# A decoder layer's MLP: the second product as seven block products instead of eight

## The chip, the cores and the metric

The kernel runs on one core of a Trainium2 chip, in float32. The time is device microseconds of one execution. The profile is one execution recorded by the hardware, and its times are counted from the first instruction.

## The reference, cut to what matters

One decoder layer on 1024 tokens of width 1024; the token mixers ahead of the MLP (an RWKV-7 recurrence and a differential attention) are left out here.

```
x = x + merged @ w_out[i]                                       # out projection
h = rmsnorm(x, norm_mlp_g[i])
x = x + jnp.square(jax.nn.relu(h @ w_ff1[i])) @ w_ff2[i]        # MLP, hidden width 4096
gate = jax.nn.sigmoid(rmsnorm(x, norm_ple_g[i]) @ w_ple_gate[i])
x = x + (p[i] @ w_ple[i]) * gate                                # gate stage
return rmsnorm(x, final_norm_g)
```

## The kernel before, in words

**Split operands.** Every large product runs on TensorE in a float32 form that keeps few bits. So each operand is split in two: `hi`, a cast by ScalarE, and `lo`, the rest, a subtraction on VectorE or GpSimd (`split`). `mm3` then issues three matmuls per pair of tiles, hi by hi, hi by lo and lo by hi, each 128x128 by 128x512.

**Order.** The code is recorded once and a scheduler places the instructions on the queue of each engine: PE (TensorE), DVE (VectorE), ACT (ScalarE), POOL (GpSimd), and SP, which issues all the DMAs. Each queue runs in its order. A tile's space is taken again once its last reader is done.

**The stages that matter.**
- *Out projection* (`out_proj`): two halves of columns, eight tiles of 128 tokens (`j`) each. In the second half `norm(j)` norms a finished tile, transposes it on TensorE into `h2`, and makes from the even tiles the operands `hb[0]` and `hb[1]` of the first MLP product, and from each pair of tiles four differences.
- *First MLP product* (`phase_ff1`): 16 pairs `g` of 128 hidden rows. The product of 2x2 blocks is already done with seven block products (Strassen's way in Winograd's form), in the order 0, 5, 1, 6, 4, 3, 2, each 12 matmuls. The moving operands `hb[i]` for i above 1 are made during pair 0 (`moving`). To cover that, products 0 and 1 of the first `AHEAD` pairs run first. The block sums go through relu and square and are stored in `dr_hid` in memory.
- *Second MLP product* (`phase_ff2`): eight groups of four tiles of 128 hidden rows. A group loads four tiles of hidden (`h0r` to `h3r`) and four of weights (`w0r` to `w3r`), splits all, and for each of the eight token tiles issues 2 halves x 4 x 3 = 24 matmuls; VectorE adds the result to `x2` (L1120).
- *Gate stage* (`phase_ple`): the gate's weights are loaded and split during the second MLP product, then each token tile in turn is normed (`normed`), multiplied, gated and stored.

Of the kernel before, what the change touches and what calls it, by code (L numbers as in the profile page):

```python
# [79 lines left out]
class Kern:  # L80
    def __init__(self, tc, A, out):
        self.tc, self.nc, self.A, self.out = tc, tc.nc, A, out
        self.raws = {}
# [79 lines left out]
    def run(self):  # L163
        nc, tc, A = self.nc, self.tc, self.A
        with ExitStack() as es:
# [13 lines left out]
            self.dr_hid = dr.tile([DFF // P, P, T], F32, name="dr_hid")  # L179
# [10 lines left out]
            with ExitStack() as right:  # L190
# [3 lines left out]
                self.f1w = opener(mid)("f1w", 5)  # L194
# [527 lines left out]
    def project(self, gw, pd, mA):  # L722
# [159 lines left out]
    def out_proj(self, pool, mA):  # L882
# [9 lines left out]
        def norm(j, xj):  # L892

            xn = self.norm_scale(xj, (nw, nw))
            nc.sync.dma_start(self.dr_x2[j, :, H:D], xj[:, H:D])
            col = lambda c: slice(c * H + j // 2 * P, c * H + (j // 2 + 1) * P)
            blk = lambda kk, c: self.h2[:, 4 * kk:4 * kk + 4, col(c)]
            for q in range(2):
# [4 lines left out]
                if j % 2 == 0:  # L903
                    self.split([t[:, :, col(0)] for t in self.hb[q]], blk(q, 0), q)
            if j % 2:
# [3 lines left out]
                sub(blk(0, 0), blk(0, 1), blk(0, 0))  # L909
                sub(t1, blk(1, 1), blk(0, 0))  # L910
                sub(blk(1, 0), blk(1, 0), t1)
                sub(blk(0, 1), blk(1, 1), blk(0, 1))

        for c in range(2):
            cols = slice(c * H, c * H + H)
            ws = [self.weights(wp, A["w_out"][k][:, cols], [P, H], "wo", lo="gv"[k % 2], raw_bufs=2) for k in range(KD)]
            for j in range(NT):
# [22 lines left out]
                if j:  # L940
# [4 lines left out]
        self.first = [self.ff1_split(self.raws[0, 0][:, 4 * i:4 * i + 4, :], i) for i in range(2)]  # L945
# [18 lines left out]

    def phase_ff1(self, pool):
# [8 lines left out]

        nc, A = self.nc, self.A
        hp, w1, wk = pool("f1h", 1), pool("f1s", 4), pool("f1k", 6)
# [7 lines left out]
        sums = lambda name, **k: wk.tile([P, H], F32, tag="o", name=name, **k)  # L984
        n = DFF // P // 2
# [12 lines left out]
        def stationary(g, order):  # L998
# [9 lines left out]
            for i in order:  # L1008
# [14 lines left out]
                yield i, self.ff1_split(src, g < 2 or i in (0, 1))  # L1023

        def store(g, m, c, src, on_scalar=False):

            o = sums("o")
            if on_scalar:
                nc.scalar.activation(o, src, AF.Relu)
                src = o  # L1030
            nc.vector.scalar_tensor_tensor(o, src, 0.0, src, op0=ALU.max, op1=ALU.mult)  # L1031
            nc.sync.dma_start(self.dr_hid[2 * g + m, :, c * H:c * H + H], o)

        def product(b, i, w, first):
            for k in range(4):
                self.mm3(b, w[0][:, k, :], w[1][:, k, :], hb[i][0][:, k, :], hb[i][1][:, k, :], first and k == 0, k == 3, not first)

        p0 = {}
        for g in range(AHEAD):
            ws = self.first if g == 0 else [self.ff1_split(raws[g, 0][:, 4 * i:4 * i + 4, :], True) for i in range(2)]  # L1040
# [5 lines left out]
            bs = [PT(), PT()]  # L1046
            for i in range(2):
                product(bs[i], i, ws[i], True)
                if i == 0:
                    p0[g] = wk.tile([P, H], F32, tag=f"p0{g}", name="p0", bufs=1)  # L1050
                    nc.scalar.copy(p0[g], bs[0])
            x = sums("x00")
            nc.vector.tensor_tensor(x, p0[g], bs[1], op=ALU.add)
            store(g, 0, 0, x)
        for g in range(n):
# [12 lines left out]
            for i, w in stationary(g, [i for i in ORDER if g >= AHEAD or i > 1]):  # L1068
# [4 lines left out]
                product(b, i, w, first)  # L1073
# [5 lines left out]
                elif i == 1:  # L1079
                    store(g, 0, 0, b, True)  # L1080
                elif i == 6:
                    plus("v", sb["u"], b)
                elif i == 4:
                    store(g, 1, 1, plus("x11", sb["v"], b))
                elif i == 3:
                    store(g, 1, 0, plus("x10", sb["u"], b))
                else:
                    store(g, 0, 1, plus("x01", sb["u"], b))

    def phase_ff2(self, pool):  # L1090

        nc, A = self.nc, self.A
        G = 4

        raw, ops = pool("f2r", 3), [pool(f"f2g{g}", 1) for g in range(2)]
        p2 = pool("f2p", 4, space=PSUM)

        def part(p, src, tag, v):
            r = raw.tile([P, D], F32, tag=tag[0] + "r", name=tag + "r")
            nc.sync.dma_start(r, src)  # L1100
            parts = [p.tile([P, D], F32R, tag=f"{tag}{n}", name=f"{tag}{n}") for n in ("hi", "lo")]
            self.split(parts, r, v)
            return parts

        n = DFF // P // G
        load = lambda g: [(part(ops[g % 2], self.dr_hid[G * g + i], f"h{i}", False), part(ops[g % 2], A["w_ff2"][G * g + i], f"w{i}", i % 2))
                          for i in range(G)]
        nxt = load(0)
        for j in range(NT):
            nc.sync.dma_start(self.x2[:, j, :], self.dr_x2[j])  # L1110
        for g in range(n):
            ws, nxt = nxt, load(g + 1) if g + 1 < n else None
            for j in range(NT):
                tok = slice(j % 2 * H + j // 2 * P, j % 2 * H + (j // 2 + 1) * P)
                pt = p2.tile([P, D], F32, tag="p2", name="p2")
                for c in range(2):
                    cols = slice(c * H, c * H + H)
                    for i, (hh, w) in enumerate(ws):
                        self.mm3(pt[:, cols], hh[0][:, tok], hh[1][:, tok], w[0][:, cols], w[1][:, cols], i == 0, i == G - 1)
                nc.vector.tensor_tensor(self.x2[:, j, :], self.x2[:, j, :], pt, op=ALU.add)  # L1120


    def phase_ple(self, pool, rpool):
        nc, A = self.nc, self.A

        wgs = [pool("plg", 1), rpool("plgr", 1)]
        left = 6
        nk, hp = pool("pln", 2), pool("plh", 2)
        wk, one = pool("plw", 2), pool("plo", 1)
# [3 lines left out]
        raw = lambda name, *shape: nk.tile([P, *shape], F32, tag="raw", name=name, bufs=3)  # L1133

        def normed(j):
            h = [hp.tile([P, KD, P], F32R, tag=f"h{i}", name=f"h{i}") for i in range(2)]
            self.norm_turn(self.norm_scale(self.x2[:, j, :], (nk, nk), raw("xn", D)), "norm_ple_g", h, (nk, nk, ps))
            return h

# [119 lines left out]
```

## Time and profile before

| | |
|---|---|
| time, median of 3 runs (lowest to highest) | 1786.38 us (1785.12 to 1790.37) |
| the profiled execution: its own time, its span | 1785.24 us, 1783.5 us |
| TensorE busy (matmuls) | 1735.6 us, 97% of the span |
| VectorE, ScalarE, GpSimd busy | 1031.8, 631.0, 388.9 us |
| mean granted TensorE clock | 0.997 of full speed |

The own time is 1.7 us above the span: what lies around the first and last instruction. An engine's busy time counts what it executes; the rest of its span it waits for another engine or a DMA.

### The profile page before, as it was taken

To read this page: it belongs to the slowest core of one execution; us is meant where nothing else is said; L and a number is where in the kernel's file an instruction comes from. 1 tells how busy PE (TensorE), PEld (TensorE's weight loads), DVE (VectorE), ACT (ScalarE), POOL (GpSimd) and SP (SyncE) were. 2 spreads that over 40 slices of the span, in tenths; PEclk is the share of its full clock that TensorE was granted. 3 is DMA by queue.
4 is the path that set the end of the run, shared out by engine and by line. 5 is a ranking of instruction groups with operands and counts; after the bars stand their busy time and mean duration, and the time that the engine had idled before them with its cause. 6 is when DMAs were issued, how large, how long until landed. Compare 5 with 4: busy or idle time off the path is not lost. (4 is left out here: it accounts for less than half of the span.)

```text
span 1783.5 us, 24054 instructions
## 1 busy us (share of the span) xinstructions
PE 1735.6 (97%) x9002; PEld 1424.3 (80%) x9002; DVE 1031.8 (58%) x2051; ACT 631.0 (35%) x1196; POOL 388.9 (22%) x321
## 2 busy tenths in 40 slices
PE   7999999999999999999999999999999999999998
PEld 7778877878877887788777778888878888888787
DVE  6357576676576564867547986566543333332653
ACT  5231452352353254766223422222231111112432
POOL 4000011010010010111502033333373333334000
PEclk9999999999999999999999999999999999999999
DMA  4323222221322318642543233333293222203101
GB/s 160 96 71 117 74 77 83 66 77 54 95 78 67 112 72 241 221 130 84 189 159 107 95 124 119 113 101 119 89 337 123 95 95 95 95 24 118 48 36 47
DMA packets 98276, 191.66 MB, mean 107 GB/s; under 512 B 34032, under 2 KB 35056, under 8 KB 98160
## 3 DMA queue, kind: packets, MB, share of 16 engines
q1 hardware_dynamic: 98160, 190.13, 32.4%
q8 instruction: 71, 1.16, 0.3%
q14 instruction: 45, 0.37, 0.1%
HBM read 138.19 MB, written 51.90 MB: 107 GB/s over the span
## 5 line engine op out<-in xcount | busy, mean ns | idle before, releaser
L158 PE MATMUL pd<-hT,w_hi 128*128 128x512 f32 (+1 forms) x688 | 274.4, 399 | 1.8 <-DVE stlo L333 1.6
L160 PE MATMUL pd<-hT,w_lo 128*128 128x512 f32 (+1 forms) x688 | 269.0, 391 | 0.0
L159 PE MATMUL pd<-hT,w_hi 128*128 128x512 f32 (+1 forms) x688 | 268.8, 391 | 0.0
L1120 DVE TENSOR_TENSOR x<-x,p 128x1024 f32<-128x1024 f32 x64 | 78.1, 1221 | 206.6 <-PE p L160 206.5
L158 PEld LDWEIGHTS pd<-hT,w_hi 128*128 128x128 f32 x688 | 129.9, 189 | 26.2 <-DVE stlo L333 2.0
L160 PEld LDWEIGHTS pd<-hT,w_lo 128*128 128x128 f32 x688 | 129.7, 188 | 24.2 <-issue 0.2
L159 PEld LDWEIGHTS pd<-hT,w_hi 128*128 128x128 f32 x688 | 129.9, 189 | 22.8 <-issue 1.0
L628 POOL COPY XV<-vt 64x128 f32<-64x128 f32 x64 | 21.0, 328 | 461.9 <-PE ps L642 365.5
L953 POOL TENSOR_TENSOR wlo<-s,whi 128x512 fp32r<-128x512 f32 x56 | 75.8, 1356 | 185.6 <-ACT whi L952 185.6
L152 DVE TENSOR_TENSOR w_lo<-w_raw,w_hi 128x1024 fp32r<-128x1024 f32 x42 | 51.3, 1221 | 72.3 <-ACT w_hi L151 71.9
L952 ACT CAST whi<-s 128x512 fp32r<-128x512 f32 x64 | 39.5, 622 | 120.6 <-PE p L159 97.6
L952 ACT CAST h0hi<-h0r 128x1024 fp32r<-128x1024 f32 x8 | 8.4, 1052 | 191.0 <-PE p L159 148.3
L151 ACT CAST w_hi<-w_raw 128x1024 fp32r<-128x1024 f32 x42 | 44.1, 1050 | 88.2 <-PE pd L159 81.8
L839 DVE CUSTOM_DVE_ANT_0 sc<-ps,tab 128x512 f32<-128x512 f32 (+3 forms) x96 | 50.7, 552 | 23.6 <-PE ps L837 23.0
L1031 DVE SCALAR_TENSOR_TENSOR o<-x 128x512 f32<-128x512 f32 x52 | 60.9, 1170 | 0.7
L952 ACT CAST whi<-w_raw 128x512 fp32r<-128x512 f32 x48 | 29.7, 622 | 83.5 <-PE p L159 75.8
L107 POOL TENSOR_TENSOR rs_r<-rs_v,mhalf 128x1 f32<-128x1 f32 (+1 forms) x32 | 28.8, 902 | 134.4 <-DVE rs_v L105 121.1
L848 ACT ACTIVATE sc<-sc,nm 128x128 f32<-128x128 f32 (+7 forms) x64 | 49.5, 776 | 13.7 <-DVE nm L846 9.0
L953 POOL TENSOR_TENSOR h0lo<-h0r,h0hi 128x1024 fp32r<-128x1024 f32 x8 | 19.4, 2424 | 158.3 <-ACT h0hi L952 158.3
L159 PE MATMUL po<-wo_lo,mh 128*128 128x512 f32 x128 | 50.2, 393 | 2.4 <-POOL wo_lo L152 2.2
L877 POOL TENSOR_TENSOR r<-e,mhalf 128x1 f32<-128x1 f32 x32 | 19.8, 619 | 149.3 <-DVE e L875 140.0
L159 PE MATMUL p<-w1lo,h1hi 128*128 128x512 f32 x128 | 49.9, 390 | 1.1 <-DVE w1lo L953 1.1
(415 smaller groups left out, 4635.9 us busy)
## 6 DMA issues: line engine op xcount, KB each, us to landing
w_raw<-w_in SPq DMA_DIRECT2D x42, 512.0 KB, 3.5
w_raw<-w_ff SPq DMA_DIRECT2D x36, 512.0 KB, 3.8
dr_hid<-o SPq DMA_DIRECT2D x64, 256.0 KB, 2.1
dr_gate<-st SPq DMA_DIRECT2D x32, 256.0 KB, 2.0
gate<-dr_gate SPq DMA_DIRECT2D x32, 256.0 KB, 2.6
xj<-x SPq DMA_DIRECT2D x8, 512.0 KB, 6.9
qs<-dr_q SPq DMA_DIRECT2D x8, 512.0 KB, 6.5
kh<-dr_k SPq DMA_DIRECT2D x16, 256.0 KB, 7.2
```

Of the source, the lines that this page charges most:

```text
L107: nc.gpsimd.tensor_tensor(r, v, self.mhalf[:, :n], op=ALU.pow)
L151: nc.scalar.copy(hi_, raw)
L152: (nc.gpsimd if lo == "g" else nc.vector).tensor_tensor(lo_, raw, hi_.bitcast(F32), op=ALU.subtract)
L158: mm(out, wh, hh, start=first, stop=False, skip_group_check=more)
L159: mm(out, wh, hl, start=False, stop=False, skip_group_check=more)
L160: mm(out, wl, hh, start=False, stop=last, skip_group_check=more)
L839: nc.vector.tensor_tensor_reduce(s[:, c0:c1], pss[:, 0:c1 - c0], tab[:, o + c0:o + c1], 1.0, NEG, op0=ALU.add, op1=ALU.max, accum_out=mx[: ...
L848: nc.scalar.activation(s[:, 0:kend], s[:, 0:kend], AF.Exp, bias=nm, scale=SLOPES[h], accum_out=t)
L952: self.nc.scalar.copy(hi, src)
L953: (self.nc.vector if on_vector else self.nc.gpsimd).tensor_tensor(lo, src, hi.bitcast(F32), op=ALU.subtract)
L1031: nc.vector.scalar_tensor_tensor(o, src, 0.0, src, op0=ALU.max, op1=ALU.mult)
L1120: nc.vector.tensor_tensor(self.x2[:, j, :], self.x2[:, j, :], pt, op=ALU.add)
```

## The change

The second MLP product becomes seven block products too. Hidden (1024 tokens by 4096) and weights (4096 by 1024) are taken as 2x2 blocks: tokens by parity of their tile, hidden rows by parity of theirs, columns by halves. The work is in 4 groups of 7 steps, one step a block product: 4 token tiles x 4 hidden tiles x 3 = 48 matmuls. The left operands are sums of blocks of hidden, which `phase_ff1` now makes and stores in `dr_hid` as seven blocks; the right operands are differences of weight blocks made on VectorE (`sub`, L1159). The results are added to `x2`, or to a running sum `u`, in pieces of 128x512. All `lo` splits of both MLP products move to VectorE, with those of the out projection's weights, of the gate's weights, and the adds of `mA` ahead of it. Relu and square of the hidden go to ScalarE, two instructions each. The operands of steps 0, 2, 4 ... (`f2o0`) and the first loads lie in space that is free since the first pair or, for `hb[0]` and `hb[1]`, since products 0 and 1 of the last pair. `AHEAD` falls from 4 to 3, and products 0 and 1 of pair 0 are issued inside `out_proj`, ahead of the last tile's norm; the norm of the tile before is issued within the last product. The gate stage takes the odd tiles first, and tile 1 is normed within the last step of the second MLP product.

```diff
-                    (nc.gpsimd if ct + 1 < KD else nc.vector).tensor_tensor(m, m, g, op=ALU.add)
+                    nc.vector.tensor_tensor(m, m, g, op=ALU.add)
...
+                    if (c, j, k) == (1, NT - 1, KD // 2):
+                        norm(j - 1, last)
...
-        self.first = [self.ff1_split(self.raws[0, 0][:, 4 * i:4 * i + 4, :], i) for i in range(2)]
+        ws = [self.ff1_split(self.raws[0, 0][:, 4 * i:4 * i + 4, :], True) for i in range(2)]
+        self.ff1_load(1)
+        self.ahead(0, ws, [pd.tile([P, H], F32, tag="pd", name="po") for i in range(2)], xp.tile([P, H], F32, tag="xh", name="x00"))
         norm(NT - 1, last)
...
-        AHEAD = 4
+        AHEAD = 3
...
-                yield i, self.ff1_split(src, g < 2 or i in (0, 1))
+                yield i, self.ff1_split(src, True)
...
-                    store(g, 0, 1, plus("x01", sb["u"], b))
+                    x = plus("a01", sb["u"], b)
+                    a[0, 1] = self.relu2(x, x, True)
+                    s2 = sums("s2")
+                    sub(s2, a[0, 0], x)
+                    store(6, s2)
+                    nc.vector.tensor_tensor(x, x, a[1, 1], op=ALU.add)
+                    store(4, x)
+                    sub(a[0, 0], x, a[0, 0])
+                    store(5, a[0, 0])
+                    sub(a[1, 0], a[1, 0], a[0, 0])
+                    store(2, a[1, 0])
...
+        def operands(step):
...
+            for q in range(KB):
+                if i == 5:
+                    sub(tmp["t0"], b01, b00, q)
+                    sub(src, b11, tmp["t0"], q)
+                elif i == 6:
+                    sub(b01, b11, b01, q)
+                elif i == 3:
+                    sub(b10, b10, tmp["t1"], q)
+                self.split([t[:, q, :] for t in mp], src[:, q, :], True)
+                self.split([t[:, q, :] for t in sp], h[:, q, :], True)
+            return sp, mp
...
+        for step in range(7 * n):
+            g, i = step // 7, ORDER[step % 7]
+            (sp, mp), nxt = nxt, operands(step + 1) if step + 1 < 7 * n else None
...
+            for p in range(NT // 2):
...
+                for q in range(KB):
+                    self.mm3(b, sp[0][:, q, tok], sp[1][:, q, tok], mp[0][:, q, :], mp[1][:, q, :], share is None and q == 0, q == KB - 1, share is not None)
...
+                nc.vector.tensor_tensor(to, to, b, op=ALU.add)
...
+                if step == 7 * n - 1 and p == 1:
+
+                    self.h1 = self.normed(1, first, first, lambda: ps.tile([P, H], F32, tag=f"p{(step + 1) % 2}", name="pt"), 1)
```

**SP's queue where the first MLP product ends.** Rows `dr_hid<-` are stores of the last pairs' hidden (before: `o`; now `a00`, `a11`, `a10`, `a01`, `s2`). Before, the loads for the second MLP product (`h0r`, `w0r`, ...) stand among the stores:

```order
L1032 DMA dr_hid_71<-o_11651 128x512
L1100 DMA h0r_11826<-dr_hid_71 128x1024
L1032 DMA dr_hid_71<-o_11712 128x512
L1100 DMA w0r_11832<-w_ff2 128x1024
L1100 DMA h1r_11838<-dr_hid_71 128x1024
L1100 DMA w1r_11844<-w_ff2 128x1024
L1032 DMA dr_hid_71<-o_11756 128x512
L1100 DMA h2r_11850<-dr_hid_71 128x1024
```

Now (`b00` to `b10` are the weight blocks of group 0, 1 MB each; the hidden of steps 0 and 1 stands some 40 to 50 rows earlier):

```order
L1086 DMA dr_hid_71<-a00_11882 128x512
L1167 DMA h_12132<-dr_hid_71 128x4x512
L1086 DMA dr_hid_71<-a11_11924 128x512
L1086 DMA dr_hid_71<-a10_11945 128x512
L1156 DMA b00_12014<-w_ff2 128x4x512
L1156 DMA b01_12018<-w_ff2 128x4x512
L1086 DMA dr_hid_71<-s2_11972 128x512
L1086 DMA dr_hid_71<-a01_11968 128x512
L1086 DMA dr_hid_71<-a00_11882 128x512
L1086 DMA dr_hid_71<-a10_11945 128x512
L1156 DMA b11_12020<-w_ff2 128x4x512
L1156 DMA b10_12022<-w_ff2 128x4x512
```

Before, the first weights (`w0r`) were loaded after one of the last pair's stores with three to come; now `b00` stands behind the store of `a10`, the result of the last product but one, and `b11` and `b10` behind the pair's last store.

**PE where the out projection ends.** `po<-wo` is the out projection, `pt<-cs,nrm_xn` the eight transposes of a normed tile, `hb0` and `hb1` the first MLP product. Before:

```order
L158 MATMUL po<-wo_hi,mh 128x512
L159 MATMUL po<-wo_lo,mh 128x512
L160 MATMUL po<-wo_hi,ml 128x512
L99 MATMUL pt<-cs,nrm_xn 128x128 x16
L158 MATMUL p_9303<-hb0hi,whi 128x512
```

Now (fifteen rows of `po<-wo` of the last tile, the same three five times, stand ahead of these transposes):

```order
L99 MATMUL pt<-cs,nrm_xn 128x128 x8
L158 MATMUL po<-wo_hi,mh 128x512
L159 MATMUL po<-wo_lo,mh 128x512
L160 MATMUL po<-wo_hi,ml 128x512
L158 MATMUL po<-wo_hi,mh 128x512
L159 MATMUL po<-wo_lo,mh 128x512
L160 MATMUL po<-wo_hi,ml 128x512
L158 MATMUL po<-wo_hi,mh 128x512
L159 MATMUL po<-wo_lo,mh 128x512
L160 MATMUL po<-wo_hi,ml 128x512
L158 MATMUL po<-hb0hi,whi 128x512
```

The transposes of the last tile but one moved into the last product; those of the last tile moved behind 24 matmuls of the first MLP product.

**DVE in the second MLP product.** Before (`x<-x,p` is the add of a token tile):

```order
L1120 TENSOR_TENSOR x_11813<-x_11813,p_13136 128x1024
L953 TENSOR_TENSOR w1lo<-w1r,w1hi 128x1024
L1120 TENSOR_TENSOR x_11813<-x_11813,p_13210 128x1024
L953 TENSOR_TENSOR w3lo<-w3r,w3hi 128x1024
L1120 TENSOR_TENSOR x_11813<-x_11813,p_13236 128x1024
```

Now, one step (`slo`, `mlo`: splits for the next step; `b<-b,t`: a difference of weight blocks; `u<-u,p`: the adds of this step's four token tiles):

```order
L972 TENSOR_TENSOR slo_13263<-h_13260,shi_13262 128x512
L972 TENSOR_TENSOR mlo_13265<-b10_13098,mhi_13264 128x512 x2
L972 TENSOR_TENSOR slo_13263<-h_13260,shi_13262 128x512
L972 TENSOR_TENSOR mlo_13265<-b10_13098,mhi_13264 128x512
L972 TENSOR_TENSOR slo_13263<-h_13260,shi_13262 128x512
L972 TENSOR_TENSOR mlo_13265<-b10_13098,mhi_13264 128x512
L972 TENSOR_TENSOR slo_13263<-h_13260,shi_13262 128x512
L1207 TENSOR_TENSOR u_12007<-u_12007,p2_13282 128x512
L1207 TENSOR_TENSOR u_12007<-u_12007,p2_13296 128x512
L1159 TENSOR_TENSOR b10_13098<-b10_13098,t1_13179 128x512 x3
L1207 TENSOR_TENSOR u_12007<-u_12007,p2_13310 128x512
L1159 TENSOR_TENSOR b10_13098<-b10_13098,t1_13179 128x512
```

Each step has eight splits, then four adds, with the differences in between. In the whole of the second MLP product DVE now has 224 splits, 64 differences and 120 adds of 128x512, 408 in all; POOL has none there.

## Rows read from the trace of the kernel before

**Rows 1.** The page, part 1: busy us, share of the span, instructions.

```profile
PE 1735.6 (97%) x9002; PEld 1424.3 (80%) x9002; DVE 1031.8 (58%) x2051; ACT 631.0 (35%) x1196; POOL 388.9 (22%) x321
```

**Rows 2.** Windows: us, PE, PEld, DVE, ACT, POOL busy, clock, DMA.

```profile
1160.00:1300.00 140.00, 140.00 (x620) 115.91 (x619) 86.32 (x104) 39.87 (x65) 51.56 (x37) 1.00 0.34 113
1320.00:1640.00 320.00, 320.00 (x1413) 264.98 (x1412) 111.04 (x76) 65.43 (x66) 132.85 (x51) 1.00 0.30 107
```

**Rows 3.** Waits of PE from 850 us: in total, times, longest.

```profile
PE pt L99 <- DVE nrm_xn L122: 5.9, 3, 4.0
PE po L159 <- POOL wo_lo L152: 2.2, 2, 1.4
PE p L158 <- DVE x L1065: 1.9, 2, 1.1
PE p L159 <- DVE w1lo L953: 1.1, 1, 1.1
PE pt L99 <- DVE nrm_ht L138: 1.0, 1, 1.0
PE pg L160 <- DVE h L141: 1.0, 1, 1.0
...
PE pg L158 <- ACT h L140: 0.4, 1, 0.4
PE p L159 <- POOL w2lo L953: 0.4, 1, 0.4
```

**Rows 4.** DVE, by form, from 870 us: busy, mean ns.

```profile
L953 DVE TENSOR_TENSOR w1lo<-w1r,w1hi 128x1024 fp32r<-128x1024 f32 x8 | 23.8, 2970 | 3.2 <-ACT w1hi L952 3.2
...
L1005 DVE TENSOR_TENSOR s<-s,w_raw 128x512 f32<-128x512 f32 x16 | 19.5, 1219 | 1.1
...
L953 DVE TENSOR_TENSOR wlo<-s,whi 128x512 fp32r<-128x512 f32 x8 | 5.3, 688 | 0.2 <-ACT whi L952 0.2
```

**Rows 5.** Timeline of DVE and ACT in pair 0: start, us.

```profile
1010.41 1.15 ACT L952 CAST hb5hi<-t 128x512 fp32r<-128x512 f32 x2
...
1020.18 1.89 DVE L953 TENSOR_TENSOR hb3lo<-h,hb3hi 128x512 fp32r<-128x512 f32 x3
```

**Rows 6.** Timeline where the out projection ends.

```profile
986.64 1.03 PE L99 MATMUL pt<-cs,nrm_xn 128*128 128x128 f32 x8
...
989.76 1.26 POOL L953 TENSOR_TENSOR hb0lo<-h,hb0hi 128x512 fp32r<-128x512 f32 x1
...
991.72 1.94 PE L99 MATMUL pt<-cs,nrm_xn 128*128 128x128 f32 x8 [4.04 <-DVE nrm_xn L122]
```

**Rows 7.** Windows behind that wait; columns as in rows 2.

```profile
988.00:992.00 4.00, 0.28 (x2) 0.31 (x3) 3.06 (x5) 1.94 (x4) 1.78 (x2) 0.71 0.17 66
992.00:996.00 4.00, 4.00 (x14) 3.45 (x13) 3.13 (x6) 0.00 (x0) 0.00 (x0) 0.50 0.00 0
996.00:1000.00 4.00, 4.00 (x18) 3.29 (x17) 2.65 (x5) 2.80 (x6) 0.00 (x0) 0.94 0.00 0
```

**Rows 8.** Timeline where the first MLP product ends.

```profile
1299.50 0.69 DVE L1065 TENSOR_TENSOR x<-u,p 128x512 f32<-128x512 f32 x1 [1.31 <-PE p L160]
...
1301.49 0.32 SPq L1032 DMA_DIRECT2D dr_hid<-o  x1
...
1301.79 0.39 PE L160 MATMUL p<-hb2hi,wlo 128*128 128x512 f32 x1
1303.05 1.17 PE L158 MATMUL p<-w0hi,h0hi 128*128 128x512 f32 x4 [0.87 <-DVE x L1065]
```

**Rows 9.** DMA issues: count, KB each, median us to landing.

```profile
gate<-dr_gate SPq DMA_DIRECT2D x32, 256.0 KB, 2.6
...
h0r<-dr_hid SPq DMA_DIRECT2D x8, 512.0 KB, 3.3
...
x<-dr_x SPq DMA_DIRECT2D x8, 512.0 KB, 7.9
...
pin<-p SPq DMA_DIRECT2D x2, 512.0 KB, 3.8
```

More of the change, by code (lines that the diff above doesn't have):

```diff
@@ L963, in ff1_split, with relu2, product, ahead @@
         return w
+    def relu2(self, o, src, on_scalar=False):
+        nc = self.nc
+        if on_scalar:
+            nc.scalar.activation(o, src, AF.Relu)
+            nc.scalar.activation(o, o, AF.Square)
+        else:
+            nc.vector.scalar_tensor_tensor(o, src, 0.0, src, op0=ALU.max, op1=ALU.mult)
+        return o
+    def product(self, b, i, w, first):
+        hi, lo = self.hb[i]
+        for k in range(4):
+            self.mm3(b, w[0][:, k, :], w[1][:, k, :], hi[:, k, :], lo[:, k, :], first and k == 0, k == 3, not first)
+    def ahead(self, g, ws, bs, x, pool=None):
+        nc = self.nc
+        for i in range(2):
+            self.product(bs[i], i, ws[i], True)
+            if i == 0:
+                p0 = self.p0[g] = (pool or self.f1w).tile([P, H], F32, tag=f"p0{g}", name="p0", bufs=1)
+                nc.scalar.copy(p0, bs[0])
+        nc.vector.tensor_tensor(x, p0, bs[1], op=ALU.add)
+        nc.sync.dma_start(self.dr_hid[0, g], self.relu2(x, x, True))
     def phase_ff1(self, pool):
         nc, A = self.nc, self.A
-        hp, w1, wk = pool("f1h", 1), pool("f1s", 4), pool("f1k", 6)
+        hp, w1, wk = pool("f1h", 1), pool("f1s", 4), pool("f1k", 9)
         ps = pool("f1p", 8, space=PSUM)
@@ L1022, in stationary @@
                     src = add("s3", r(1, 0), tmp["s1"], ALU.subtract)
-                yield i, self.ff1_split(src, g < 2 or i in (0, 1))
[L1025 to L1040, printed above, removed]
+                yield i, self.ff1_split(src, True)
+        for g in range(1, AHEAD):
+            ws = [self.ff1_split(raws[g, 0][:, 4 * i:4 * i + 4, :], True) for i in range(2)]
             if g + 1 < AHEAD:
@@ L1045, in phase_ff1 @@
                     self.ff1_load(0, m)
[L1046 to L1054, printed above, removed]
+            self.ahead(g, ws, [PT(), PT()], sums("x00"), wk)
         for g in range(n):
@@ L1083, in phase_ff1 @@
                 elif i == 4:
-                    store(g, 1, 1, plus("x11", sb["v"], b))
+                    x = plus("a11", sb["v"], b)
+                    a[1, 1] = self.relu2(x, x, True)
+                    store(3, x)
                 elif i == 3:
-                    store(g, 1, 0, plus("x10", sb["u"], b))
-                else:
-                    store(g, 0, 1, plus("x01", sb["u"], b))
-    def phase_ff2(self, pool):
-        nc, A = self.nc, self.A
[L1093 to L1120, printed above, removed]
@@ new lines, in phase_ff1 @@
+                    x = plus("a10", sb["u"], b)
+                    a[1, 0] = self.relu2(x, x, True)
+                    store(1, x)
+                else:
+                    x = plus("a01", sb["u"], b)
[9 more added lines that the diff above has]
+                    store(2, a[1, 0])
@@ L1132, in phase_ple @@
         pw = pool("plpw", 2, space=PSUM)
[L1133 to L1138, printed above, removed]
+        raw = lambda name, *shape: rp.tile([P, *shape], F32, tag="raw", name=name)
+        normed = lambda j: self.normed(j, nk, hp, lambda: ps.tile([P, H], F32, tag="ps", name="pt"))
         ws, pins = [], []
@@ L1150, in phase_ple @@
             nc.sync.dma_start(pins[q], A["p"][q * H:(q + 1) * H, :].rearrange("(j p) (k c) -> p j k c", p=P, k=2))
-        wp = [self.weights(one, A["w_ple"][k], [P, D], f"wple{k}", lo="v", raw_tag="wple_raw", raw_bufs=2) for k in range(2)]
+        wp = []
+        for k in range(2):
+            w = raw("wple_raw", D)
+            nc.sync.dma_start(w, A["w_ple"][k])
+            wp.append([one.tile([P, D], F32R, name=f"wple{k}{n}") for n in ("hi", "lo")])
+            self.split(wp[k], w, True)
         gf = one.tile([P, D], F32, name="gf")
@@ L1192, in phase_ple @@
                 nc.scalar.activation(t[:, cols], pgt, AF.Tanh, scale=0.5)
-            if j == 0:
+            if n == 0:
                 embed()
```

137 lines of the change are left out of this document (107 added, 30 removed).

## The prediction

> **What bounds the kernel now.** I read the page first, for the engine that sets the end: TensorE is busy for 97% of the span [rows 1], so time comes only from fewer matmuls or from its waits. Next the windows, for the price of one matmul. 620 matmuls in 140 us of the first MLP product and 1413 in 320 us of the second, at a clock of 1.00, are one per 0.226 us in both [rows 2]. I take 0.2265. VectorE is busy for only 111 of those 320 us, ScalarE for 65, GpSimd for 133. Then the waits, for what a change of order can win. From the out projection on, the longest is 4.0 us, on a normed tile ahead of the first MLP product; the rest are small, and together they come to some 14 us [rows 3]. Then the forms and the timeline of VectorE, for what the work that moves there will cost [rows 4, 5], and the timelines of the places where the order changes [rows 6, 8], with the granted clock behind the long wait [rows 7] and the DMAs' landing times [rows 9].
>
> The sum is made against the profiled execution's own time, 1785.2 us (the median of the runs is 1.1 above).
>
> **The change part by part.**
>
> *Fewer matmuls.* The second product issues 8 groups x 8 token tiles x 2 halves x 4 x 3 = 1536 matmuls now, and 28 steps x 48 = 1344 after: 192 fewer, of the same shape. At 0.2265 that is **-43.5**. The Trainium skill (page "TensorE: Matmul & The Clock Gate", section "Wait — 56ns, not 53.3ns?") gives back-to-back matmuls of 512 columns a spacing of 215.7 ns at full clock. By that the term would be -41.4 (an estimate from that page), and the result 2.1 later. The rows show the longer spacing over thousands of these matmuls, so the measured one stands.
>
> *Work costed at nothing.* The cover is the 1344 x 0.2265 = 304.4 us of matmuls. Under it VectorE has 408 instructions of 128x512. Splits of that size run in a row at 1.89 / 3 = 0.63 us, the last one's end included, and start 0.60 apart [rows 5]. At 0.605 the 408 take 247 us, 81% of the cover; at 0.688, the mean of one form without GpSimd beside it [rows 4], 281 us, 92%. I take the first, since splits in a row are what most of it is. ScalarE has 224 casts at 1.15 / 2, below 0.6 each [rows 5]: under 135 us. Within a step of 48 x 0.2265 = 10.9 us the eight splits for the next step come first in VectorE's queue, so the operands are ready some 5 us ahead. In the first product, a pair of 84 x 0.2265 = 19.0 us covers some 20 VectorE instructions (12.1 us), and ScalarE's 16 casts, relus and squares (10 us). If the cover failed, each us of VectorE beyond 10.9 in a step would be a us of TensorE's wait.
>
> *Hidden through memory.* Seven blocks instead of four are stored and loaded. Each step needs one load of 1 MB in 10.9 us, issued a step ahead; 512 KB land in 3.3 us [rows 9]. Nothing.
>
> *Out projection's weights.* Half of the `lo` splits leave GpSimd, for which TensorE waits 2.2 us in two places [rows 3]. VectorE takes them in half the time or less. **-1.5** (0 if the loads then end last, -2.2 if all goes).
>
> *Start of the first product.* Now TensorE waits 4.04 us for `nrm_xn` [rows 6] and then runs at a clock of 0.50 for 4 us, at 0.71 and 0.94 around that [rows 7]; half of 4 us plus a little is 2.2 lost. With 24 matmuls (5.4 us) put between, the wait is covered and the clock has no reason to fall: -6.2. Against that, these matmuls need `hb0lo`, whose GpSimd half takes 1.26 us behind the transposes [rows 6]: +1.0. And with one product pair fewer ahead, pair 0 and the two pairs' products ahead of it are 108 matmuls, 24.5 us, while VectorE has 44 instructions there (sums and splits of the other five `hb`, weights): 26.6 us at 0.605. It is 2.1 late, and the first operand of pair 1, queued behind, some 1.9 more: 4.0 in place of 1.1 now (`w1lo` [rows 3]): +2.9. Net **-2.3**. Bounds: -7.3 if VectorE keeps up and the half is in time; at 0.688 the 44 take 30.3 us, 5.8 + 1.8 late: +1.6 or so.
>
> *Entry of the second product.* Now TensorE waits 0.87 us before its first matmul [rows 8], and 1.1 and 0.4 behind it [rows 3]: 2.4. After, the first left operand is ready early, but the first right operand `b00` (1 MB) stands on SP's queue behind the store of `a10`, the result of the last product but one. That product ends 12 x 0.2265 = 2.7 us before the first MLP product does (E). Its add takes 0.7 us [rows 8] and starts at once; relu and square on ScalarE take 0.6 each; so the store goes out at about E-0.6, and behind its 0.3 us of issue [rows 8] `b00` at E-0.2. Landing: 256 KB take 2.6 us and 512 KB 3.3 [rows 9], 0.7 per 256 KB, so 1 MB takes 4.7, and I take 5.0 since `b01` and stores share the engines. Then a cast of 0.6: the first matmul comes at E+5.5. The first `lo` adds 0.5. The pause is longer than the 4.04 one, behind which the clock stood at 0.50, so another 1.5 is lost. 7.5 in all: **+5.1**. Bounds: with 3.3 for the load (the nearest measured) and no fall of the clock, 4.3, so +1.9; with the 7.9 of loads that stand eight in a row [rows 9], 10.9, so +8.5. A load of one block on a nearly empty queue is nearest to the first kind.
>
> *Start of the gate stage.* Now 1.0 + 1.0 + 0.4 = 2.4 of waits [rows 3]. After, the transposes of the first tile lie inside the last step, so the first two waits go. But the raw buffers of `pin` (512 KB, 3.8 us [rows 9]) come free only once the gate's weights are split, and VectorE has about 24 us of work in the last two steps' 21.7: eight splits of 128x1024 at twice the 128x512 price, 9.7 us; eight of 128x512, eight adds and two norms for the rest. So `pin` lands about 1.7 late, and smaller waits on the second tile and on `h` add as much again: 3.4, **+1.0** (bounds -1.4, if the loads are in time; +4, if the second `pin` is late by its full 3.8 too).
>
> *Sum.* -43.5 - 1.5 - 2.3 + 5.1 + 1.0 = -41.2, so **1744.0 us**. Within this case the bounds of the terms, which hardly all fall on one side, give 1737 to 1751.
>
> **The rivals.**
>
> (A) *The new starts are hidden* (0.13). `b00` lands under the last product, pair 0 keeps up, `pin` is in time: -43.5 - 1.5 - 5.2 (the late half of `hb0` stays) + 1.0 - 1.0, about -50: 1735. For it: the space of `b00` has been free since the first pair. Against it: SP's order, in which the load stands behind a store that can't go out before E-0.6.
>
> (B) *VectorE is short in single steps* (0.15). The step ahead of product 5 holds 8 splits, 8 differences and 4 adds: 20 x 0.605 = 12.1 us against 10.9; at 0.688, 13.8. In the last group further adds into `x2` come in. Where what is late isn't won back in the neighbouring steps, each of the four groups loses 3 to 5 us: 12 to 20 in all, 1756 to 1764. For it: the average leaves only 19% free, or 8% at the higher price. Against it: splits come ahead of adds in the queue, so a late add holds only a PSUM bank, and each bank has a step's time to spare.
>
> (C) *Slower: VectorE becomes the bound of the second product* (0.03). It decides once an instruction takes longer than (304.4 + 41.2) / 408 = 0.85 us. At the 1.219 us that a 128x512 form takes while GpSimd works beside it [rows 4] the 408 take 497 us: 193 over the cover, about 1937. For it: GpSimd is busy for 133 of 320 us in that stretch now, and 128x1024 splits take 2970 ns there. Against it: GpSimd has no splits left in that stretch, so the cause of the high price goes with the move.
>
> (D) *TensorE does no less work* (0.02), if the recorded matmuls were replaced elsewhere: about 1786. TensorE's order shows 192 rows fewer, so hardly.
>
> **How the numbers follow.** The forecast has a chance of 0.67 and gives the time, 1744. A measurement of this kernel tells from no change about 0.3%, 5 us. All of the forecast, A and B lie more than that below 1786, so faster has 0.94 (0.67 + 0.13 + 0.15, less a point for what none of the cases holds), the same 0.02 (D), slower 0.04 (C and that point). For 8 in 10 the range takes in the forecast's own range, most of A, and the near edge of B, since a short VectorE may cost in one group only: 1735 to 1758.
>
> **What would show it.** Right: 1344 matmuls of the second product 0.2265 apart, with almost no wait of TensorE between them; VectorE's splits of 128x512 some 0.60 apart there; one wait of about 5.5 us on the DMA of `b00` before the first of them, with the granted clock at 0.5 behind it; no wait of 4 us on `nrm_xn`; some 4 us of waits on VectorE's splits in pairs 0 and 1; 1 to 2 us on `pin` where the gate stage starts. Wrong: waits on `slo` or `mlo` at the start of each step (B, or C if their price is above 0.85 us); no wait on `b00` (A). The forecast depends most on the price of a VectorE instruction beside ScalarE's casts and TensorE's weight loads at this density, which the trace of before shows in short stretches only.

## The result: 1739.7 us

| | before | now |
|---|---|---|
| time, median (lowest to highest) | 1786.61 us (1785.12 to 1790.37) | 1739.70 us (1739.07 to 1741.09) |
| span of the profiled execution | 1783.5 us | 1738.0 us |
| ratio of the times, 95% interval | | 0.9735 [0.9723, 0.9746] |

The forecast was 1744.0 in a range of 1735 to 1758: the time lies inside it, 4.3 us below the value. The page's part 1 of the changed kernel (busy us, share, instructions), against [rows 1]:

```profile
PE 1691.8 (97%) x8810; PEld 1387.1 (80%) x8810; DVE 1179.9 (68%) x2487; ACT 763.5 (44%) x1492; POOL 112.3 (6%) x172
```

192 matmuls fewer, 43.8 us less of TensorE, and GpSimd nearly empty. Windows within the second product, against [rows 2] (us, then busy time of PE, PEld, DVE, ACT, POOL with instructions, clock, DMA share, GB/s), and a form of VectorE there (mean ns at the end), against [rows 4]:

```profile
1330.00:1600.00 270.00, 270.00 (x1193) 223.56 (x1192) 222.58 (x364) 108.54 (x200) 1.10 (x2) 1.00 0.42 143
```

```profile
L972 DVE TENSOR_TENSOR slo<-h,shi 128x512 fp32r<-128x512 f32 x100 | 68.3, 685 | 0.0
```

One matmul per 0.2263 us and no wait in 270 us. VectorE is busy for 82%: 222.58 / 364 = 0.611 us an instruction. The waits of TensorE from 850 us, against [rows 3]:

```profile
PE p L158 <- ACT mhi L971: 5.5, 1, 5.5
PE pt L99 <- DMA pin<-p: 2.0, 2, 1.0
PE p L158 <- ACT whi L971: 1.6, 2, 1.1
PE pt L99 <- DVE nrm_xn L908: 0.9, 1, 0.9
PE po L159 <- POOL hb0lo L972: 0.8, 1, 0.8
PE pt L99 <- DVE nrm_v L905: 0.8, 1, 0.8
PE p L160 <- DVE wlo L972: 0.7, 2, 0.4
```

The 4.0 us on `nrm_xn` are gone, and so is GpSimd's `wo_lo`; one new wait of 5.5 us stands out. (Not quite all `lo` splits of the MLP went to VectorE, as the section on the change has it: GpSimd still makes `hb0lo` of the even tiles, with the wait of 0.8 us.) The timeline at its place, the entry of the second product (start, us), against [rows 8]:

```profile
1294.44 0.39 PE L160 MATMUL p<-hb2hi,wlo 128*128 128x512 f32 x1
1294.57 1.05 SPq L1156 DMA_DIRECT2D b<-w_ff  x2
...
1296.63 0.62 ACT L989 ACTIVATE a<-a 128x512 f32<-128x512 f32 x1
1297.17 0.60 ACT L971 CAST shi<-h 128x512 fp32r<-128x512 f32 x1
...
1299.70 2.18 ACT L971 CAST mhi<-b 128x512 fp32r<-128x512 f32 x4 [1.93 <-DMA b<-w_ff]
1300.37 1.22 PE L158 MATMUL p<-mhi,shi 128*128 128x512 f32 x2 [5.54 <-ACT mhi L971]
```

SP issues `b00` 0.1 us after the first product's last matmul has started, it lands 5 us later, ScalarE casts it, and TensorE starts. Behind it, in windows, the half clock of [rows 7]:

```profile
1300.00:1304.00 4.00, 3.63 (x8) 2.65 (x9) 3.10 (x5) 1.88 (x4) 0.00 (x0) 0.50 1.02 319
1304.00:1308.00 4.00, 4.00 (x19) 3.25 (x18) 1.90 (x3) 0.68 (x2) 0.00 (x0) 1.00 1.05 408
```

Where the 45.5 us of span went, by the starts of the same matmuls in the two timelines:

| stretch | before | now | difference |
|---|---|---|---|
| start to the first `po` matmul | 886.67 | 884.76 | -1.9 |
| first `po` to the first product's first matmul | 106.64 | 97.89 | -8.8 |
| first product, first to last matmul | 308.48 | 311.79 | +3.3 |
| to the second product's first matmul | 1.26 | 5.93 | +4.7 |
| second product, first to last matmul | 350.16 | 307.75 | -42.4 |
| to the end | 130.29 | 129.88 | -0.4 |

### The profile page after: what moved, and what is told of

Same layout as the page of the kernel before. It is cut to its first block, busy times and chain, and to the rows that moved or that the text cites. A ratio compares the mean times of both kernels' runs of the same rounds, so it can differ in the third digit from the quotient of the medians.

```text
span 1738.0 us, 24124 instructions
## 1 busy us (share of the span) xinstructions
PE 1691.8 (97%) x8810; PEld 1387.1 (80%) x8810; DVE 1179.9 (68%) x2487; ACT 763.5 (44%) x1492; POOL 112.3 (6%) x172
## 4 chain that ended last, share of the span: by engine, by line
PE 84%; DVE 7%; issue 3%; ACT 3%; POOL 2%; DMA 1%; SPq 0%; POOLq 0%; DVEq 0%; ACTq 0%
PE p L158 11%; PE p L160 11%; PE p L159 11%; PE pd L158 10%; PE pd L159 10%; PE pd L160 10%; PE ps L643 2%; PE pg L160 1%; PE pg L158 1%; PE pg L159 1%; PE pS L497 1%; PE pt L870 1%; PE pt L99 1%; PE pyg L606 1%; PE po L159 1%
## 5 line engine op out<-in xcount | busy, mean ns | idle before, releaser
L158 PE MATMUL p<-mhi,shi 128*128 128x512 f32 x448 | 175.2, 392 | 5.5 <-ACT mhi L971 5.5
L159 PE MATMUL p<-mlo,shi 128*128 128x512 f32 x448 | 175.1, 391 | 0.0
L160 PE MATMUL p<-mhi,slo 128*128 128x512 f32 x448 | 174.8, 390 | 0.0
L971 ACT CAST shi<-h 128x512 fp32r<-128x512 f32 x112 | 68.5, 617 | 158.9 <-PE p L159 145.9
L158 PEld LDWEIGHTS p<-mhi,shi 128*128 128x128 f32 x448 | 84.4, 189 | 23.7 <-ACT mhi L971 6.4
L159 PEld LDWEIGHTS p<-mlo,shi 128*128 128x128 f32 x448 | 84.5, 189 | 18.5 <-DVE mlo L972 0.9
L160 PEld LDWEIGHTS p<-mhi,slo 128*128 128x128 f32 x448 | 84.4, 188 | 17.5
L972 DVE TENSOR_TENSOR slo<-h,shi 128x512 fp32r<-128x512 f32 x112 | 76.4, 686 | 0.7 <-ACT shi L971 0.7
L1207 DVE TENSOR_TENSOR x<-x,p 128x512 f32<-128x512 f32 x80 | 53.1, 683 | 32.8 <-PE p L160 32.8
L972 DVE TENSOR_TENSOR mlo<-b,mhi 128x512 fp32r<-128x512 f32 x80 | 53.2, 686 | 0.8 <-ACT mhi L971 0.8
```

Of the source, the lines that this page charges most:

```text
L158: mm(out, wh, hh, start=first, stop=False, skip_group_check=more)
L159: mm(out, wh, hl, start=False, stop=False, skip_group_check=more)
L160: mm(out, wl, hh, start=False, stop=last, skip_group_check=more)
L971: self.nc.scalar.copy(hi, src)
L972: (self.nc.vector if on_vector else self.nc.gpsimd).tensor_tensor(lo, src, hi.bitcast(F32), op=ALU.subtract)
L1207: nc.vector.tensor_tensor(to, to, b, op=ALU.add)
```

## The experiments

The start to the first `po` matmul took between 883.4 and 887.8 us over these runs, also where its code was the same. So beside the times I compare stretches behind it. "Head" is from the first `po` matmul to the first product's last (409.7 us in the changed kernel), "tail" from there to the end of the span (443.6 us). Where I say in which steps a run loses time, it is by the starts of the same matmuls in two timelines. Ratios are to the kernel before, with an interval of about 0.0015 either way; the changed kernel has 0.9735.

**1. `b00` loaded early.** One load moves from SP's queue to GpSimd's.

```diff
-            nc.sync.dma_start(t, A["w_ff2"][...])
+            (nc.gpsimd if (g, f, c) == (0, 0, 0) else nc.sync).dma_start(t, A["w_ff2"][...])
```

> The load of the first weight block b00 stands on GpSimd's queue instead of SP's, so it goes out while the first MLP product still runs; everything else stays. In the changed kernel TensorE waits 5.5 us at the entry of the second product, and some 2 us more go at the half clock behind it. If the landing of b00 alone holds the entry, the wait is gone and the time falls by about 7.5 us, to 1732. My theory: the cast of b00 then stands on ScalarE behind the last relu, square and cast of the first product (they end 3 us after its last matmul), so the first matmul comes about 3.5 us after the last one of the first product, only 2 us earlier: 1738 (the clock may still fall).

Ratio 0.9747, 1740.3 us; tail 444.0. The waits in the timeline:

```profile
1301.46 0.73 PE L158 MATMUL p<-mhi,shi 128*128 128x512 f32 x2 [3.51 <-ACT mhi L971]
1304.49 0.79 PE L159 MATMUL p<-mlo,shi 128*128 128x512 f32 x1 [2.29 <-DVE mlo L972]
```

The first wait fell to 3.5 us, as my theory had it, but a second of 2.3 us on VectorE's `mlo` took its place, which I had not priced: on VectorE too the operand stood behind the last pair's sums. Nothing was gained.

**2. `b00` split on GpSimd as well.**

```diff
+                    nc.gpsimd.tensor_copy(mp[0][:, q, :], src[:, q, :])
+                    nc.gpsimd.tensor_tensor(mp[1][:, q, :], src[:, q, :], mp[0][:, q, :].bitcast(F32), op=ALU.subtract)
```

> As the run before, and the cast and the subtraction of b00 are made on GpSimd too, which is idle there and can begin once products 0 and 1 of the last pair are done. If load and cast are all that holds the entry, the wait is below 0.5 us, the granted clock stays at 1.00, and the time falls by 7 us or a little more, to about 1732.5. Rival: the wait only moves, to the second step, whose blocks b01 and b11 are loaded where they were: then its first matmul waits 2 to 5 us and half of the gain or more is lost, 1735 to 1738.

0.9745, 1740.7 us; tail 444.0: the rival held, and took all of the gain. The entry's wait is down to 0.87 us, and six short ones stand in step 2. VectorE's timeline there, and windows:

```profile
1304.04 1.29 DVE L1159 TENSOR_TENSOR t<-b,b 128x512 f32<-128x512 f32 x2 [1.34 <-DMA b<-w_ff]
1307.72 1.30 DVE L1159 TENSOR_TENSOR t<-b,t 128x512 f32<-128x512 f32 x2 [2.40 <-DMA b<-w_ff]
```

```profile
1305.00:1310.00 5.00, 4.32 (x18) 3.00 (x16) 2.60 (x5) 1.55 (x3) 0.00 (x0) 1.00 1.04 399
1310.00:1315.00 5.00, 3.11 (x9) 1.63 (x9) 5.00 (x10) 2.40 (x6) 0.00 (x0) 0.94 1.03 418
1315.00:1320.00 5.00, 4.64 (x11) 3.44 (x11) 5.00 (x10) 4.12 (x9) 0.00 (x0) 0.50 1.02 419
```

`b01` and `b11`, issued at 1296.6, land at 1304.0 and 1307.7, with the DMA engines full (share above 1.0, some 400 GB/s). The second step's differences come late, and in the stretch of short waits the clock falls all the same.

**3 and 4. Two and four more VectorE instructions per step**, subtractions of 128x512 whose results nobody reads.

```diff
+        extra = pool("f2x", 2)
...
+                if q >= 2:      # run 4: every q
+                    nc.vector.tensor_tensor(extra.tile([P, H], F32, tag="x", name="extra"), h[:, q, :], h[:, q, :], op=ALU.subtract)
```

> Two subtractions of 128x512 more per step on VectorE (results unused), 464 instead of 408 in the second product. If VectorE's work is hidden as a sum over steps (0.61 us each, 283 us under 304), the time stays within 1 us of 1739.7. If single steps are short already (rival B of the prediction), the step ahead of product 5 with 22 instructions (13.4 us against 10.9) and its neighbours lose 2 to 5 us in each of the four groups: 1748 to 1760.

> Four subtractions more per step on VectorE, 520 in all. At 0.61 us they take 317 us, 13 over the 304 of matmuls, so VectorE becomes the bound of the second product by a little: about 1750 to 1753, with waits of TensorE on slo and mlo. If the price of an instruction falls in a dense row, or matmuls lose nothing, 1740; if VectorE is slowed by the density, above 1760.

Two more: 0.9746, 1741.4 us, tail 445.9. Four more: 0.9843, 1758.2 us, tail 462.4. The windows of the two runs, in that order:

```profile
1330.00:1600.00 270.00, 270.00 (x1193) 223.58 (x1192) 252.02 (x415) 108.91 (x202) 0.55 (x1) 1.00 0.41 141
```

```profile
1330.00:1600.00 270.00, 266.65 (x1164) 219.70 (x1163) 266.44 (x442) 107.02 (x196) 0.00 (x0) 0.99 0.39 134
```

Run 3: at 93% VectorE costs TensorE nothing in these 270 us, the same 1193 matmuls start. Its 2 us are lost in the first two steps (a wait of 0.9 us on `mlo` is new there) and stay the same from then on; so the time is 1.7 us above 1739.7, where I had allowed 1.

Run 4: VectorE is full, 266.44 / 442 = 0.603 us an instruction, but that alone doesn't hold TensorE. One window of a group's length, the place of the only wait in the middle, and the window around it:

```profile
1406.00:1482.00 76.00, 76.00 (x337) 62.92 (x336) 75.64 (x126) 30.54 (x56) 0.00 (x0) 1.00 0.42 143
```

```profile
1592.37 2.07 PE L158 MATMUL p<-mhi,shi 128*128 128x512 f32 x4 [3.35 <-ACT mhi L971]
```

```profile
1590.00:1600.00 10.00, 7.63 (x22) 6.11 (x23) 9.65 (x17) 5.64 (x11) 0.00 (x0) 0.66 0.01 2
```

In the three windows of 76 us from 1330 us on, VectorE is busy for 98 to 99.5%, and 337, 337 and 336 matmuls start, where the changed kernel starts 337 in each. Then, in the last group, one wait of 3.35 us and the lower clock behind it cost 6.6 us. Two things meet there: a group needs 128 VectorE instructions and 125 or 126 are done in 76 us, so VectorE falls behind a little in each; and the last group has 12 more, the adds of `u` into `x2`. Four of them, among eight adds from 1585.0 to 1589.8 us, stand in VectorE's queue just ahead of the differences that the late operand is made of. This reading is argued from the order and the counts; no run takes the adds out. The time rose by more than the 10 to 13 us expected: to the second product's first matmul it takes 2.6 us longer, the second product's matmuls 6.5, and what VectorE puts off comes due in the gate stage, which is 9.7 us longer (seven waits of 0.3 to 2.3 us there, on the first token tile's operand, on `pT` and on splits of the gate stage's weights, and a clock of 0.83 in two windows of 10 us).

**5. The whole entry.** `b00` as in run 2, the other three blocks from GpSimd's queue early, `mlo` in between, and the loads of `x2` behind the second step's operand.

```diff
+                nc.gpsimd.tensor_copy(t[:, 0, 0:1], after)              # b01, b11, b10: behind the casts of b00
+            (nc.sync if g else nc.gpsimd).dma_start(t, A["w_ff2"][...])
...
-                    nc.sync.dma_start(self.x2[:, j, :], self.dr_x2[j])
+                    nc.gpsimd.tensor_copy(self.x2[:, j, 0:1], tmp["t1"][:, 3, 0:1])
+                    nc.gpsimd.dma_start(self.x2[:, j, :], self.dr_x2[j])
```

> The second run moved the wait to the second step (its first operand is the difference of three blocks, and b01 and b11 landed 7 to 11 us after their issue, while the loads of x2 and the last stores filled the DMA engines). Here b00 is loaded and split on GpSimd as there, b01, b11 and b10 are loaded from GpSimd's queue as soon as that allows, and the eight loads of x2 wait until the second step's operand is made. If the loads of the blocks are what holds the entry, TensorE's waits in the first two steps fall from 4 us to under 1.5 us, the granted clock stays at 1.00, and from the end of the first product to the end of the program there are 437 us instead of 443: 1733. If the late adds of the first product's last pair on VectorE hold it as well, 440 us.

0.9719, 1735.3 us; tail 438.3, 5.3 us shorter. The two waits that are left:

```profile
1295.88 1.17 PE L158 MATMUL p<-mhi,shi 128*128 128x512 f32 x4 [0.87 <-DVE a L1093]
1309.02 0.50 PE L158 MATMUL p<-mhi,shi 128*128 128x512 f32 x1 [0.21 <-ACT mhi L971]
```

So the entry is held by all four blocks and the work on them, not by the first load alone; its 5 us over the kernel before could be had back. Which share the late loads of `x2` have in that isn't separated.

**6 and 9. The last tile's norm ahead of pair 0's products again.** Run 6 only swaps the two calls:

```diff
+        norm(NT - 1, last)
         self.ahead(0, ws, ...)
-        norm(NT - 1, last)
```

> One part of the change undone: the last tile's norm is issued ahead of products 0 and 1 of pair 0 again. If the prediction's account holds (the norm's chain of 4 us on ScalarE, VectorE and GpSimd is covered by these 24 matmuls), TensorE waits 3 to 4 us on nrm_xn again, the clock falls behind it, the 0.85 us on hb0lo goes, and the time rises by 3 to 5.5 us: 1743 to 1745. Rival: the norm in two halves is short enough by itself, and the time stays within 1 us.

0.9744, 1740.2 us; head 409.4. Nothing moved, because the scheduler put 14 of the 24 matmuls ahead of the transposes by itself: the test didn't test. Run 9 records the products in the first product's stage, in its own PSUM banks:

```diff
-        self.ahead(0, ws, [pd.tile(...) for i in range(2)], xp.tile(...))
+        self.first = ws
...
+        self.ahead(0, self.first, [PT(), PT()], sums("x00"))    # phase_ff1
```

> In the run with the norm issued first the scheduler still put 14 matmuls of pair 0 ahead of the last tile's transposes, so the part of the change was not undone. Here products 0 and 1 of pair 0 are recorded in the first product's own stage and write its PSUM banks, so they can only follow the transposes, as before the change. If the 24 matmuls are what covers the norm's chain, TensorE waits 3.5 to 4 us on nrm_xn ahead of them, the clock falls to 0.5 behind it for 2 us more, and the time rises by 4.5 to 6 us, to 1744 to 1746. If not, 1740.

0.9745, 1742.1 us (the changed kernel measured beside it: 1740.4); head 411.2. The timeline and the windows of run 9:

```profile
987.29 1.94 PE L99 MATMUL pt<-cs,nrm_xn 128*128 128x128 f32 x8 [4.90 <-DVE nrm_xn L908]
```

```profile
984.00:988.00 4.00, 0.71 (x4) 0.74 (x5) 1.56 (x4) 0.72 (x2) 0.55 (x1) 0.81 0.17 66
988.00:992.00 4.00, 4.00 (x13) 3.34 (x12) 3.39 (x6) 0.03 (x1) 0.00 (x0) 0.50 0.00 0
...
1010.00:1015.00 5.00, 5.00 (x24) 4.14 (x23) 5.00 (x9) 2.32 (x5) 0.00 (x0) 1.00 0.68 233
1015.00:1020.00 5.00, 5.00 (x23) 4.14 (x23) 4.87 (x9) 2.71 (x5) 0.00 (x0) 1.00 0.21 81
```

The wait (4.9 us) and the half clock are back. But pair 0 then runs without a wait: 47 matmuls in 1010 to 1020 us, where the changed kernel starts 28:

```profile
1010.00:1015.00 5.00, 4.06 (x15) 2.20 (x13) 5.00 (x10) 2.46 (x4) 0.00 (x0) 1.00 0.61 197
1015.00:1020.00 5.00, 3.48 (x13) 2.03 (x13) 4.97 (x9) 2.45 (x6) 0.00 (x0) 1.00 0.31 118
```

VectorE is full in both. The part is worth 1.5 to 2 us, not the 4.5 to 6 that I expected here: what TensorE doesn't wait for the norm it waits for VectorE's work 25 us later.

**7. Adds of `mA` and half of the out projection's `lo` splits back on GpSimd.**

```diff
-                    nc.vector.tensor_tensor(m, m, g, op=ALU.add)
+                    (nc.gpsimd if ct + 1 < KD else nc.vector).tensor_tensor(m, m, g, op=ALU.add)
...
-            ws = [... "wo", lo="v", raw_bufs=2 ...]
+            ws = [... "wo", lo="gv"[k % 2], raw_bufs=2 ...]
```

> Two parts undone, apart in the program: the adds of mA and half of the out projection's lo splits go back to GpSimd. The prediction took 1.5 us for the splits and nothing for the adds. Then TensorE waits some 2 us on GpSimd's wo_lo again, the stretch of the 230 matmuls ahead of the out projection stays at 53.5 us, and the time rises by 1.5 to 2.5 us. If the adds matter too, that stretch takes 54.7 us as before the change, and the rise is 3 us or more.

0.9772, 1745.3 us; head 412.8. Between the first `po` matmul and the first product's first there are 101.17 us, 3.3 more. Windows of the matmuls ahead of that, for the changed kernel and for this run:

```profile
835.00:886.00 51.00, 51.00 (x221) 41.11 (x220) 37.66 (x63) 14.73 (x29) 0.00 (x0) 1.00 0.62 196
```

```profile
835.00:886.00 51.00, 50.35 (x214) 39.28 (x213) 28.99 (x43) 13.23 (x28) 27.52 (x19) 1.00 0.54 175
```

Seven matmuls fewer start in 51 us. By the starts of the same 230 matmuls ahead of the first `po`, it is 55.2 us against 53.5, 1.7 us (54.7 in the kernel before, 1.1 us). So this stretch does matter, which the prediction had at nothing. The adds and the first half's `lo` splits both stand in it on GpSimd, and this run doesn't separate them.

The 3.3 us behind it lie in one place, where the second half's weights come in. The table of waits has 1.6 us there, 0.2 on VectorE and 1.4 on GpSimd's `wo_lo`:

```profile
933.19 0.50 PE L158 MATMUL po<-wo_hi,mh 128*128 128x512 f32 x1
935.06 0.79 PE L159 MATMUL po<-wo_lo,mh 128*128 128x512 f32 x1 [1.37 <-POOL wo_lo L152]
935.65 0.63 PE L160 MATMUL po<-wo_hi,ml 128*128 128x512 f32 x1
936.08 0.63 PE L158 MATMUL po<-wo_hi,mh 128*128 128x512 f32 x1
```

```profile
936.00:940.00 4.00, 4.00 (x14) 3.13 (x13) 0.54 (x2) 1.24 (x2) 1.29 (x1) 0.69 0.37 132
```

The rest is of two kinds. From the start at 933.19 to the one at 935.06 are 1.87 us, 1.64 more than the usual spacing, where the row names 1.37: it counts only from the end of the matmul before, which the profile puts 0.5 us behind its start. And behind the wait the clock is down and six matmuls start 0.43 us apart, which costs some 1.6 us in all. In the kernel before, the clock stays at 1.00 there, and the same stretch is 3.2 us longer than now, by waits alone (2.5 us by their rows). So the splits are worth twice what I took.

**8. The left operands' `lo` splits back on GpSimd.**

```diff
-                self.split([t[:, q, :] for t in sp], h[:, q, :], True)
+                self.split([t[:, q, :] for t in sp], h[:, q, :], False)
```

> The left operands' lo splits of the second product (112 of 408 instructions) go back to GpSimd. If what the prediction took from the trace of before holds, that a VectorE instruction of 128x512 takes up to 1.2 us beside GpSimd, then VectorE's other 296 cost some 0.75 to 1.0 us each (222 to 296 us) and the step's four GpSimd splits 1.3 to 3 us each (5 to 12 us in a step of 10.9): from no change to 30 us slower, with waits of TensorE on slo. If GpSimd and VectorE do not hinder each other, VectorE is at 0.61 us, GpSimd at 1.3 or less, and the time is 1740 or, if VectorE's load mattered, a little below.

0.9766, 1744.0 us; tail 447.1. VectorE's forms between 1330 and 1600 us:

```profile
L972 DVE TENSOR_TENSOR mlo<-b,mhi 128x512 fp32r<-128x512 f32 x72 | 86.6, 1236 | 2.1 <-ACT mhi L971 2.1
L1207 DVE TENSOR_TENSOR x<-x,p 128x512 f32<-128x512 f32 x74 | 49.1, 677 | 17.1 <-PE p L160 16.6
```

A subtraction goes from 0.69 to 1.24 us; the add that reads PSUM, where TensorE's results land, stays at 0.68. VectorE is busy for 241.66 of 270 us with 262 instructions, where it was for 222.58 with 364: taking a quarter of its work away made it busier. It is still hidden in the middle of the stage: between the 97th and the 1000th matmul nothing is lost. Of the 3.5 us by which the tail is longer, 2.7 are lost in the first two steps (7.9 us of waits, where 5.5 stood) and 1.0 in the last group; what the wait on `pin` (the tiles of `p` that the gate stage loads) costs is won back behind it. The Trainium skill ("SBUF — State Buffer", section "Who interferes with whom") says this: a VectorE instruction with two SBUF inputs contends with a GpSimd instruction that reads SBUF, one with at most one SBUF input, outside the modes that use both of VectorE's port pairs, doesn't. The two rows agree with it: a split has two inputs in SBUF, the add takes one from PSUM.

**10. `AHEAD` 4 again**, with eight buffers for sums instead of nine.

> AHEAD is 4 again (with eight buffers for sums instead of nine), so 24 more matmuls cover the sums and splits that pair 0 needs. In the changed kernel 16 matmuls too few start between 1010 and 1020 us, 3.6 us. If VectorE's 44 instructions there are the cause, these waits go (2.3 us by the table of waits, up to 3.6) and the time falls to 1736 to 1737.5. If the lost buffer holds TensorE elsewhere, no change.

0.9715, 1737.0 us, 3.4 below the changed kernel measured beside it; head 406.0 against 409.4. Of that, 2.4 us lie in the first product's first 240 matmuls, where it was expected; the rest is a wait of 0.9 us on `nrm_xn` that isn't there; why it went, the run doesn't show.

**11. Together:** run 5, run 10, and `hb0lo` of the normed tiles on VectorE. **12.** The changed kernel again.

> The fifth run's entry of the second product (5 us), AHEAD 4 (2 to 3.6 us) and the last tile's hb0lo on VectorE instead of GpSimd (up to 0.85 us) together. If they add up: 1730 to 1732, against 1739.7 of the changed kernel.

> The changed kernel itself beside the other three on the same chip, to compare them directly: 1739.7, give or take 1.5.

Run 12 gave 1740.4 us (0.9736). Run 11 gave 0.9692, 1733.0 us: 7.4 us faster than the changed kernel and 55.3 us faster than the one before on the same chip, some 2 us short of the sum. The entry's wait is gone altogether, but the gate stage lost 2.4 us to new waits:

```profile
PE pt L99 <- DMA pin<-p: 2.6, 2, 1.3
PE pt L99 <- DVE pT L1283: 2.4, 1, 2.4
```

Why VectorE's `pT` comes later there was not tried.

## Why the prediction was right, and where it was off

| term | predicted | measured |
|---|---|---|
| fewer matmuls and entry of the second product | -38.4 | -37.7 |
| out projection's weights, from the first `po` matmul on | -1.5 | -3.3 (run 7) |
| adds of `mA`, with the splits beside them | not priced | -1.1 (run 7: -1.7) |
| start of the first product | -2.3 | -2.2 |
| start of the gate stage | +1.0 | -0.4 |
| start of the program, code unchanged | 0 | -0.8 |
| sum | -41.2 | -45.5 |

(The eight transposes that moved from the gate stage into the last step, 0.8 us, stand in the first line as measured. Counted where the prediction has them, the first line is -38.5 and the gate stage +0.4.)

*Fewer matmuls, at 0.2265.* Right: 0.2263 now. The matmuls are as far apart as before, so the term is their number. The Trainium skill (page "TensorE: Matmul & The Clock Gate", section "Wait — 56ns, not 53.3ns?") gives 215.7 ns for such a spacing; these runs show the longer one.

*The cover.* Right in price (0.611 against 0.605 us) and in share (82% against 81%). So rival B, single steps that are short, is refuted for this kernel: with two instructions more in every step, 22 ahead of product 5, the same number of matmuls start (run 3). A step's lateness is won back in the next. Run 4 shows where the cover ends: not at a share (98 to 99% of VectorE is free of cost for three groups), but in the last group, whose further adds rival B named. Rival C's mechanism is real (run 8), and to leave it out was right: without GpSimd the tail is 3.5 us shorter.

*Entry of the second product.* Right in its main parts: `b00` behind the store of `a10`, the first matmul 5.5 us after the first product's end (5.5 of wait), the clock at 0.50, 7.5 lost in all (5.93 to the first matmul, and about 2 at half clock; the 0.5 for `mlo` did not come, and the clock cost 0.5 more than was taken). The upper bound was summed wrongly: with 7.9 in place of 5.0 for the load it is 10.4 and +8.0, not 10.9 and +8.5. But the prediction named only `b00`; its "Nothing" for memory counts one load a step and leaves out the other three blocks of a group. Runs 1, 2 and 5 show that the next things stand right behind it: the cast and the subtraction behind the last pair's work on ScalarE and VectorE, and the other blocks behind full DMA engines. Rival A ("`b00` lands under the last product") would not have given its 1735 by that alone.

*Start of the first product.* The net was right to 0.1, -2.2 (in the two stretches of the table -8.8 and +3.3, less the weights' -3.3). Its parts were too: the wait for the norm gone, 0.85 for `hb0lo`, and pair 0 short of VectorE (16 matmuls too few in 10 us, 3.6 us, where 4.0 was said). Run 9 shows that two terms which the prediction adds hang together: with the pause back, the shortage is gone, since VectorE gets ahead in the pause (it ends the four splits `hb3lo` 127.7 us after the first `po` matmul, as in the changed kernel with 127.8, but TensorE comes to them at 131.3 instead of 125.5). A fourth pair ahead takes most of the shortage away too, without the pause (run 10). (At 0.688 the bound of this term comes to +1.3, not +1.6.)

*Where it was off.* Two sizes, both of work that left GpSimd. "VectorE takes them in half the time or less. -1.5" counted only the waits that the table named (2.2 us); run 7 puts the splits at 3.3, and in the kernel before the same stretch is 3.2 us longer than now: a wait costs more than its row, and in run 7 the clock falls behind it too. And the adds of `mA` were listed in the change and priced nowhere; the table of waits shows 0.2 us there in the kernel before, where 1.1 was lost. At the gate stage the waits on `pin` came as said (2.0 us), but the smaller ones came to 0.7 where 1.7 was taken; that is read from the trace, no run tests it. The 0.8 us at the start of the program no run pins down: its length differs by more than that between runs of the same code. Counted as in the note under the table, these misses lie on one side, so the forecast did not hit by large errors that cancel; it was 4.3 us too careful.

## What to carry to other kernels

Where TensorE sets the time, count how many matmuls start in a window rather than add up its waits: part of each wait shows as "busy", the clock may be down behind it, and work taken off GpSimd was worth more than its waits showed. When one late operand holds the start of a stage, look at every queue and transfer behind it before pricing its removal; here the load, the cast, the subtraction and three more loads each stood ready to take its place. An engine that is full need not hold the one that sets the time, as long as its lead lasts; look at the last group, where extra work comes in. And a scheduler may have made an edit of the code's order already: look at the order it gives before spending a run on it.

## What the runs showed of the hardware

Taking work from VectorE to GpSimd can make VectorE busier: 262 instructions took 241.66 us in run 8, 364 took 222.58 without GpSimd. The price sits on instructions with both inputs in SBUF (0.69 to 1.24 us), while those that read PSUM stay (0.68 us).

TensorE's granted clock fell to 0.50 in run 2 with no wait above 0.7 us in the 15 us around it: six waits of 0.3 to 0.7 us, 18, 9 and 11 matmuls in three windows of 5 us. A row of short waits can cost more than their sum. It need not: in the changed kernel 15 and 13 matmuls start between 1010 and 1020 us at a clock of 1.00. And the same wait of 1.37 us on `wo_lo` has the clock at 0.69 behind it in run 7 and at 1.00 in the kernel before.
